# Filter MLP ahead of the modulation, and butterflies cut into an even and an odd part

## The chip, the cores and the metric

The kernel runs on one core of one Trainium2 chip. Its time is device time in microseconds; the time before is the median of three runs.

## The reference

One inference step of a two-layer backbone of width 1024 over 1024 sample tokens and 128 prompt tokens. Layer 0 mixes with gated linear attention and retention, layer 1 with a Hyena long convolution and a gated linear recurrence. Each layer's input is an RMSNorm of the tokens, scaled and shifted by a modulation that comes from the conditioning vectors (`silu(cond) @ w_mod + b_mod`).

The part that matters here is the Hyena filters. A small MLP (33 position features, then 64 and 64 hidden units, each with a sine) gives hidden units at every tap; a last layer and an exponential window make four filters of 1024 channels:

```python
def long_conv(u, hf_fwd, hf_bwd, skip):
    uf = jnp.fft.rfft(u, n=2 * L, axis=1)
    y = jnp.fft.irfft(uf * (hf_fwd + jnp.conj(hf_bwd))[None], n=2 * L, axis=1)[:, :L]
    return y + u * skip
```

The filters depend on weights alone, not on tokens, so the kernel works out their spectra first.

## The kernel before

The kernel runs in phases: phase 0 the filters' spectra, the modulation and layer 0's normalised input; phase 1 layer 0's heads; phase 2 its output projection; phase 3 layer 1's convolutions and recurrence; phase 4 its output projection. Every phase but 0 is unchanged.

A tiling framework turns the traced program into one instruction list per engine. It keeps dependences, and orders what is ready by priority, which is the order of the trace unless `high_priority(n)` lifts a block. So an instruction can move ahead of one traced earlier, but on the chip each engine then runs its list in order. `issue_after(ins)` adds an edge: every instruction that the block traces on the engine of `ins` comes behind `ins`; instructions on other engines are free. DMAs are issued from the lists of SP, ACT or POOL.

Phase 0 starts with small loads on SP (`setup`, `windows`, `mlp_loads`, `filter_weights`, `vectors`). `mlp_loads` brings the MLP's vectors (hv), its first weights (w1), the features (ft) and its second weights (w2). `filter_mlp` multiplies them (tiles `tr` in PSUM), reduces the argument on VectorE in `fold` (tiles sv, sk) and takes sines on ScalarE (tiles g); the high and low parts go to GA and GB. `table` places a load of an activation table set behind all sines. `vectors` loads a table of columns, transposes it on TensorE and copies it on VectorE (cols). `modulation` is a generator: each step multiplies one slab of w_mod (loaded from POOL into seven buffers, wm and wr); twelve steps run here, and others are put between the leaves later. `windows` makes 18 exponentials of [128, 256] (win) for each group of 256 channels.

`filters` then treats eight convolutions n (four channel groups, two filters each). For one convolution, `taps` makes 18 blocks of [128, 256] in nine PSUM tiles (`mm`, four banks in rotation, products wa x GA and wb x GB) and multiplies each by the window into `fa` on VectorE. The sum and the difference of the halves of fa, and then `butterfly`, all on VectorE, make 16 leaves: the even ones (k = 0, 2, 4, 6; k = 8 is the prompt's and needs no butterfly) from the sums, the odd ones (k = 1, 3, 5, 7) from the differences (fd). Then nine `leaf` products (mm<-fa,fw: eight TensorE instructions each) are evicted by ScalarE to fH and stored to h_dram by SP. The taps of convolution n + 1 are traced between the butterfly and the leaves of n.

Beside this, `others[n]` runs in four convolutions: n = 0 `start` (squares of nine tiles of tokens, loaded from ACT's queue into xs, for the norm's scale), n = 1, 2 and 7 `h_tiles` of three token tiles each (load x, scale, transpose on TensorE, modulate to htmp, split into hh and hl). Between leaves, in all but n = 1, one or two steps of the modulation are placed.

Of the kernel before, what the change touches and what calls it, by code (L numbers as in the profile page):

```python
# [17 lines left out]
P = 128  # L18
# [28 lines left out]
# rows of the column table: name -> (first column, number of columns)  # L47
# [18 lines left out]
def constants():  # L66
    """Arrays that depend on shapes alone."""
# [35 lines left out]
    # prompt: length 256  # L103
# [65 lines left out]
class Step:  # L169
# [53 lines left out]
    def sto2(self, out, in_):  # L223
        """a store that no load waits behind"""
        return self.nc.gpsimd.dma_start(out, in_)
# [5 lines left out]
    def rstd(self, pool, ms, shape, tag, scale=1.0):  # L231
        """(ms * scale + eps) ** -0.5 with one Newton step"""
        v = self.t(pool, shape, tag + "v")
        r = self.t(pool, shape, tag + "r")
        q = self.t(pool, shape, tag + "q")
        self.ts(v, ms, scale, OP.mult, EPS, OP.add)
        self.act(r, v, AF.Ln)
        self.act(r, r, AF.Exp, scale=-0.5)
        self.tt(q, r, r, OP.mult)
        self.tt(q, q, v, OP.mult)  # L240
        self.ts(q, q, -0.5, OP.mult, 1.5, OP.add)
        self.tt(r, r, q, OP.mult)
        return r

# [25 lines left out]
    def vectors(self, p, ps):  # L270
        """the table of columns"""
# [23 lines left out]
    def silu_sig(self, a, l, x):  # L295
        """a = sigmoid(x) = exp(min(x, 0) - ln(1 + exp(-|x|)))"""
# [7 lines left out]
    def modulation(self, layer, p, psm, js=(0, 8), more=None):  # L304
        """columns js (by 384) of the modulation as rows, and its columns once the scales are there"""
# [49 lines left out]
    def gate_row(self, layer, r, p, ps, tag="po", gate=None):  # L355
        """the gate along every partition, [P, D]"""
# [16 lines left out]
    def norm_tile(self, p, x, junk, out, tag="n"):  # L373
        """out = x * rstd"""
# [5 lines left out]
    def mod_transpose(self, ps, layer, t, xn, dst):  # L380
        """dst [P, KT, P] = (xn * A + B)^T"""
# [16 lines left out]
    def fold(self, p, v, out, tag):  # L398
        """out = sin(v); v is lost"""
# [8 lines left out]
    def table(self, name, after):  # L408
        """one load of an activation table set, behind the instructions `after`"""
# [8 lines left out]
    def mlp_loads(self, pt):  # L418
# [7 lines left out]
        self.ld(w1, i["hy_w1"][0])  # L426
        self.ld(ft, i["k_feat"])
        w2 = self.t(pt, [P, 2, 64], "w2")
        for e in range(2):
            self.ld(w2[64 * e:64 * e + 64], i["hy_w2"][0].unsqueeze(1).to_broadcast([64, 2, 64]))  # L430
        return hv, w1, ft, w2

    def filter_mlp(self, p, pt, ps, loads):
        """the hidden units of the filters' MLP at all taps, for products in two passes: their high
        and low parts on top of each other, and the high parts on rows of ones. A last block has
        the first tap alone, which only the forward filter takes."""
# [29 lines left out]
        for e in range(2):  # L466
            h = slice(64 * e, 64 * e + 64)
            for c in range(2):
# [10 lines left out]
                for z, (a, b) in enumerate(((lo, min(hi, DEC)), (DEC, hi))):  # L479
                    if a >= b:  # L480
                        continue
                    # taps a .. b - 1, then in reverse behind a first one of zero
# [8 lines left out]
    def butterfly(self, p, L, xe, xo, C):  # L491
        """the radix-16 stage: L = (the odd leaves c1, c3, c5, c7; the two of c0 and c8, then c2, c4, c6)
        from the even and odd inputs [P, 8, C]; xe may be the odd leaves' place"""
        L, E = L
# [12 lines left out]
        stt(E[:, 6:8], mp, -R2, M, d4[:, 0:4:2], A)  # L507
        w1 = self.t(p, [P, 4, C], "bs")
# [22 lines left out]
    def leaf(self, out_r, out_i, L, k):  # L531
# [9 lines left out]
        # FSIGN > 0: (C, S, -S) ; else (C, -S, -C)  # L541
# [9 lines left out]
    def windows(self, pt, g):  # L551
# [4 lines left out]
        delta = self.t(pt, [P, C], "delta")  # L556
        self.ld(delta, self.i["k_delta"][:, g * C:(g + 1) * C])
        self.win = self.t(pt, [P, 18, C], "win")
        for q in range(18):
            self.act(self.win[:, q], delta, AF.Exp, scale=self.negt[:, q:q + 1])  # L560

    def filter_weights(self, pt, n, g, o):
        """the window (once per channel group) and the last layer's weights in parts"""
# [27 lines left out]
    def filters(self, p, pi, pt, G, ps, w, others, first, rest):  # L591
        """spectra of both long convolutions, to h_dram [conv, block, f, 20 x 128]"""
        C = 256

        def taps(w):
            """the windowed taps [P, 18, C] of one convolution and channel group; the skip is a part
            of the first tap"""
# [12 lines left out]

        todo = [(g, o) for g in range(D // C) for o in range(2)]
        a = taps(w)
        self.load_fw(p)
        for n, (g, o) in enumerate(todo):
            d = self.t(pi, [P, 8, C], "fd")
            self.tt(d, a[:, 0:8], a[:, 8:16], OP.subtract)
            s = a[:, 0:8]
            self.tt(s, a[:, 0:8], a[:, 8:16], OP.add)
            L = (a[:, 0:8], a[:, 8:16])
            prompt = a[:, 16:18]  # L620
            self.butterfly(pi, L, s, d, C)
            if n + 1 < len(todo):
                a = taps(self.filter_weights(pt, n + 1, *todo[n + 1]))
            if n in others:
                others[n]()
            for k in (0, 8, 1, 2, 3, 4, 5, 6, 7):
# [5 lines left out]
                if k < 8:  # L632
                    self.leaf(pm[:, :C], pm[:, C:], L, k)
                else:
                    for e in range(2):
# [4 lines left out]
                self.nc.scalar.copy(H[:, :, :2].rearrange("p b r c -> p r b c"),  # L640
                                    pm.rearrange("p (r b c) -> p r b c", r=2, b=2))
# [4 lines left out]
                self.h_store(o, g, 0 if k == 0 else 3 if k == 8 else 4 + 2 * k, H[:, :, :m])  # L646
            for z in first:
# [12 lines left out]
    def phase0(self):  # L660
# [5 lines left out]
        with ExitStack() as st:  # L666
            po = self.pool(st, "p0o", side="right")
            self.table("natural_log_exp_and_others", [])
            self.setup(po)
# [7 lines left out]
            s2 = ExitStack()  # L677
            pa = self.pool(s2, "p0a")
            self.windows(pt, 0)
            loads = self.mlp_loads(pa)  # L680
            w = self.filter_weights(pt, 0, 0, 0)
            with self.tc.high_priority(200):
                G = self.filter_mlp(pt, pa, pst, loads)
            self.vectors(pa, pst)
            first = self.modulation(0, po, psm, (0, 6), pa)
            for z in range(12):
                next(first)
            ctx = self.st.enter_context(self.tc.issue_after(self.table("natural_log_exp_and_others", self.sins).ins))

# [38 lines left out]
    def wload(self, p, src, n, width=256, tag="w", bufs=2):  # L728
        """src [D, n] -> its two float32r parts [P, KT, n], in pieces of 128 columns"""
# [9 lines left out]
    def mm3(self, out, a, b, n=KT):  # L739
        """out = sum_k a_k^T b_k for a, b each (high, low); the product of the low parts is below  # L740
        float32's last place"""
# [7 lines left out]
    def proj_et(self, ps, w, e0, ne, evac, chunks=range(3)):  # L749
        """[e, t] products: evac(chunk, psum [ne, CH])"""  # L750
# [6 lines left out]
    def phase1(self):  # L757
        i = self.i
        with ExitStack() as st:
# [21 lines left out]
            # the low-rank gates' parts on top of each other: high, low, high  # L781
# [70 lines left out]
    def proj_te(self, w, t):  # L852
        """psum [t, e] of a tile of 128 tokens"""
# [5 lines left out]
    def gate_logs(self, hh):  # L859
        """GLA: -16 (b - b_mid) for both directions, and the tiles' decays"""  # L860
# [38 lines left out]
    def gates(self, logs, q, k):  # L899
        """GLA: q and k times exp(+-(b - b_mid)) for both directions"""  # L900
# [15 lines left out]
    def decays(self, hh, q, k):  # L916
        """retention: q with the decays since the tile's start in both directions"""
# [12 lines left out]
    def sweeps(self, h, qk, scal, v):  # L930
        """the states ahead of every tile in both directions, as the products with q take them"""
# [747 lines left out]
```

## Time and profile before

| | |
|---|---|
| median of three runs | 2481.63 us (2478.56 to 2486.62) |
| profiled execution, first to last instruction | 2485.6 us |
| mean granted clock of TensorE | 0.991 |
| busy: TensorE, VectorE, ScalarE | 2418.8, 1660.5, 1070.5 us |
| phase 0, to the first unbroken products of layer 0 | 294.55 us |

The profiled execution is one of its own; its span is given, no other time. In the rows PE is TensorE's matmuls, PEld its weight loads, DVE VectorE, ACT ScalarE, SP the queue that issues most DMAs; a name with q (SPq, ACTq) is the issue of a DMA. PEclk is the granted clock of TensorE, 1.00 for 2.4 GHz and 0.50 for 1.2 GHz. A releaser is what ended an engine's wait.

### The profile page before, as it was taken

The page shows a single profiled execution, that of the slowest core. Times are in us where ns is not written, and L with a number is a line of the kernel's source. Part 1 is how long each engine was busy: PE and PEld are TensorE (multiplying, and loading weights), DVE is VectorE, ACT ScalarE, POOL GpSimd, SP SyncE. Part 2 cuts the span into 40 slices and gives each one's busy share as a digit, 9 for nine tenths or more (in the row PEclk, how much of TensorE's full clock was granted, in tenths as well). Part 3 has the DMA queues.
Part 4 walks back from the last instruction along what each step waited for, and adds up shares of the span by engine and source line. Part 5 has one row for each costly group of instructions (what it writes and reads, how often), then busy time and mean ns, then how long its engine had stood idle before and what let it go on. Part 6 is the DMA issues. An engine that isn't in the chain of part 4 may idle for free.

```text
span 2485.6 us, 38498 instructions
## 1 busy us (share of the span) xinstructions
PE 2418.8 (97%) x14681; PEld 2203.3 (89%) x14681; DVE 1660.5 (67%) x3970; ACT 1070.5 (43%) x2355; POOL 72.6 (3%) x149
## 2 busy tenths in 40 slices
PE   5899999999999999999999999999999999999998
PEld 2766899999999999998887999999999999998786
DVE  6887568677665465473324788888888887888632
ACT  5653556465544343353233322222222227888311
POOL 2011000000000000000000000000000000000000
PEclk8999999999999999999999999999999999999999
DMA  8677521121221221144335322122212211114431
GB/s 255 201 216 217 169 58 48 42 57 46 58 58 38 53 64 41 56 124 151 108 122 162 118 62 78 50 68 70 71 57 68 65 53 52 62 62 143 155 99 42
DMA packets 201080, 230.68 MB, mean 93 GB/s; under 512 B 13823, under 2 KB 171743, under 8 KB 200448
## 3 DMA queue, kind: packets, MB, share of 16 engines
q1 hardware_dynamic: 188496, 175.24, 23.3%
q0 software_dynamic: 11104, 48.27, 6.0%
q10 hardware_dynamic: 1296, 4.72, 0.6%
q8 instruction: 115, 1.88, 0.3%
q14 instruction: 69, 0.57, 0.1%
HBM read 172.27 MB, written 55.91 MB: 92 GB/s over the span
## 4 chain that ended last, share of the span: by engine, by line
PE 85%; DVE 6%; ACT 4%; DMA 4%; issue 1%; SPq 0%; DVEq 0%; ACTq 0%
PE pp L211 44%; PE po L211 13%; PE mm L211 5%; PE X L211 5%; PE pd L211 5%; PE o L211 3%; PE tr L215 2%; PE kv L211 2%; PE pg L211 2%; PE mod L211 1%; PE sc L211 1%; PE kv L215 1%; DMA wr<-h_dram 1%; DVE cs L200 1%; DVE cs L888 1%
## 5 line engine op out<-in xcount | busy, mean ns | idle before, releaser
L211 PE MATMUL pp<-gh,wh 128*128 128x384 f32 x1152 | 390.9, 340 | 3.1 <-ACT gh L394 2.5
L211 PE MATMUL pp<-gh,wl 128*128 128x384 f32 x1152 | 392.1, 341 | 0.0
L211 PE MATMUL pp<-gl,wh 128*128 128x384 f32 x1152 | 390.6, 339 | 0.4 <-DVE gl L200 0.4
L211 PE MATMUL pp<-wh,hh 128*128 128x256 f32 x1152 | 332.7, 289 | 0.0
L211 PE MATMUL pp<-wh,hl 128*128 128x256 f32 x1152 | 328.7, 285 | 0.0
L211 PE MATMUL pp<-wl,hh 128*128 128x256 f32 x1152 | 326.2, 283 | 0.0
L211 PE MATMUL po<-woh,yth 128*128 128x512 f32 x558 | 222.7, 403 | 2.9 <-ACT woh L394 2.8
L211 PEld LDWEIGHTS pp<-wh,hl 128*128 128x128 f32 x1152 | 221.7, 192 | 0.0
L211 PEld LDWEIGHTS pp<-gh,wh 128*128 128x128 f32 x1152 | 216.7, 188 | 4.5 <-ACT gh L394 3.1
L211 PEld LDWEIGHTS pp<-wl,hh 128*128 128x128 f32 x1152 | 220.6, 192 | 0.0
L211 PE MATMUL po<-wol,yth 128*128 128x512 f32 x558 | 220.1, 395 | 0.1
L211 PEld LDWEIGHTS pp<-wh,hh 128*128 128x128 f32 x1152 | 220.2, 191 | 0.0
L211 PE MATMUL po<-woh,ytl 128*128 128x512 f32 x558 | 218.8, 393 | 1.0 <-DVE ytl L200 1.0
L211 PEld LDWEIGHTS pp<-gh,wl 128*128 128x128 f32 x1152 | 216.7, 188 | 0.8
L211 PEld LDWEIGHTS pp<-gl,wh 128*128 128x128 f32 x1152 | 216.3, 188 | 1.2 <-DVE gl L200 0.7
L200 DVE TENSOR_TENSOR wl<-wr,wh 128x1024 fp32r<-128x1024 f32 (+1 forms) x97 | 118.0, 1217 | 120.2 <-ACT wh L394 119.5
L394 ACT CAST wh<-wr 128x1024 fp32r<-128x1024 f32 (+1 forms) x97 | 101.4, 1045 | 138.9 <-PE pp L211 138.8
L211 PEld LDWEIGHTS mm<-fa,fw 128*128 128x128 f32 x576 | 104.8, 190 | 41.1 <-issue 13.1
L211 PE MATMUL mm<-fa,fw 128*128 128x256 f32 x576 | 138.7, 388 | 0.0
L211 PE MATMUL pp<-hh,wh 128*128 128x384 f32 (+1 forms) x408 | 136.6, 335 | 0.3 <-ACT htmp L197 0.3
L211 PE MATMUL pp<-hh,wl 128*128 128x384 f32 (+1 forms) x408 | 136.7, 335 | 0.0
L211 PE MATMUL pp<-hl,wh 128*128 128x384 f32 (+1 forms) x408 | 136.5, 335 | 0.0
(323 smaller groups left out, 4892.2 us busy)
## 6 DMA issues: line engine op xcount, KB each, us to landing
wr<-in_ab_w_in_dram SPq DMA_DIRECT2D x48, 512.0 KB
wr<-in_cd_w_in_dram SPq DMA_DIRECT2D x48, 512.0 KB
H<-h_dram SPq DMA_DIRECT2D x32, 640.0 KB
wr<-in_w_mod_dram POOLq DMA_DIRECT2D x49, 384.0 KB, 4.6
h_dram<-fH SPq DMA_DIRECT2D x112, 128.0 KB
y_dram<-y SPq DMA_DIRECT2D x72, 128.0 KB
y<-y_dram SPq DMA_DIRECT2D x36, 256.0 KB
x<-in_x_sample_dram SPq DMA_DIRECT2D x16, 512.0 KB
```

Source lines behind the costliest of these rows:

```text
L200: return self.nc.vector.tensor_tensor(out=out, in0=a, in1=b, op=op)
L211: self.last_mm = self.nc.tensor.matmul(out, l, r, start=start, stop=stop)
L215: return self.nc.tensor.transpose(out, in_, self.ident)
L394: self.nc.scalar.copy(hi, x)
L888: self.nc.vector.tensor_tensor_scan(x, self.ones, x, 0.0, OP.mult, OP.add)
```

## The change

The loads of the MLP are traced first of all, and w1, ft and w2 are issued from ACT's queue. The load of the transform's matrices (fw, 1856 KB) moves from behind the first taps to ahead of the columns' and biases' loads. On TensorE the columns' transposition and the first twelve modulation steps come behind the MLP's last product. Of the first 18 windows, six are made at the start and twelve behind the table load that follows the sines.

The butterfly is two functions. In `filters`, the sums and the even part come first, then the leaves 0, 8, 2, 4, 6; then the differences and the odd part, the next convolution's taps, the other work (on ScalarE behind the last even leaf's eviction), and the leaves 1, 3, 5, 7. The even leaves now live in fd, the odd ones in fa. Elsewhere only comments go. The other use of the butterfly, in the long convolution, calls the two parts in turn.

```diff
@@ mlp_loads
-        self.ld(w1, i["hy_w1"][0])
-        self.ld(ft, i["k_feat"])
+        ld = self.nc.scalar.dma_start
+        ld(w1, i["hy_w1"][0])
+        ld(ft, i["k_feat"])
         w2 = self.t(pt, [P, 2, 64], "w2")
         for e in range(2):
-            self.ld(w2[64 * e:64 * e + 64], i["hy_w2"][0].unsqueeze(1).to_broadcast([64, 2, 64]))
+            self.last_ld = ld(w2[64 * e:64 * e + 64], i["hy_w2"][0].unsqueeze(1).to_broadcast([64, 2, 64]))
@@ butterfly
-    def butterfly(self, p, L, xe, xo, C):
-        L, E = L
+    def butterfly(self, p, L, x, C):
+        self.butterfly_even(p, L[1], x, C)
+        self.butterfly_odd(p, L[0], x, C)
+
+    def butterfly_even(self, p, E, xe, C):
         tt, stt = self.tt, self.stt
...
         stt(E[:, 2:4], mp, R2, M, d4[:, 0:4:2], A)
         stt(E[:, 6:8], mp, -R2, M, d4[:, 0:4:2], A)
+
+    def butterfly_odd(self, p, L, xo, C):
+        tt, stt = self.tt, self.stt
+        A, S, M = OP.add, OP.subtract, OP.mult
         w1 = self.t(p, [P, 4, C], "bs")
         w3 = self.t(p, [P, 4, C], "bd")
...
@@ windows
-        for q in range(18):
-            self.act(self.win[:, q], delta, AF.Exp, scale=self.negt[:, q:q + 1])
+        self.window(0, 18 if g else 6)
+
+    def window(self, a, b):
+        for q in range(a, b):
+            self.act(self.win[:, q], self.delta, AF.Exp, scale=self.negt[:, q:q + 1])
@@ filters
         todo = [(g, o) for g in range(D // C) for o in range(2)]
         a = taps(w)
-        self.load_fw(p)
         for n, (g, o) in enumerate(todo):
-            d = self.t(pi, [P, 8, C], "fd")
-            self.tt(d, a[:, 0:8], a[:, 8:16], OP.subtract)
-            s = a[:, 0:8]
-            self.tt(s, a[:, 0:8], a[:, 8:16], OP.add)
-            L = (a[:, 0:8], a[:, 8:16])
-            prompt = a[:, 16:18]
-            self.butterfly(pi, L, s, d, C)
+            E = self.t(pi, [P, 8, C], "fd")
+            L = a[:, 0:8]
+            prompt = a[:, 16:18]
+            self.tt(E, a[:, 0:8], a[:, 8:16], OP.add)
+            self.butterfly_even(pi, E, E, C)
+            evac = leaves(n, g, o, (0, 8, 2, 4, 6), E, L, prompt)
+            self.tt(L, a[:, 0:8], a[:, 8:16], OP.subtract)
+            self.butterfly_odd(pi, L, L, C)
             if n + 1 < len(todo):
                 a = taps(self.filter_weights(pt, n + 1, *todo[n + 1]))
             if n in others:
-                others[n]()
-            for k in (0, 8, 1, 2, 3, 4, 5, 6, 7):
+                with self.tc.issue_after(evac.ins):
+                    others[n]()
+            leaves(n, g, o, (1, 3, 5, 7), E, L, prompt)
             for z in first:
                 pass
@@ phase0
             self.table("natural_log_exp_and_others", [])
+            s2 = ExitStack()
+            pa = self.pool(s2, "p0a")
+            loads = self.mlp_loads(pa)
             self.setup(po)
...
-            s2 = ExitStack()
-            pa = self.pool(s2, "p0a")
             self.windows(pt, 0)
-            loads = self.mlp_loads(pa)
             w = self.filter_weights(pt, 0, 0, 0)
-            with self.tc.high_priority(200):
+            self.load_fw(p)
+            with self.tc.high_priority(200), self.tc.issue_after(self.last_ld.ins):
                 G = self.filter_mlp(pt, pa, pst, loads)
-            self.vectors(pa, pst)
-            first = self.modulation(0, po, psm, (0, 6), pa)
-            for z in range(12):
-                next(first)
+            with self.tc.issue_after(self.last_mm.ins):
+                self.vectors(pa, pst)
+                first = self.modulation(0, po, psm, (0, 6), pa)
+                for z in range(12):
+                    next(first)
             ctx = self.st.enter_context(self.tc.issue_after(self.table("natural_log_exp_and_others", self.sins).ins))
+            self.window(6, 18)
```

The new inner function `leaves(n, g, o, ks, E, L, prompt)` is the old body of the loop over k, for the leaves ks; it returns the last eviction.

## Rows read from the trace of the kernel before

**Rows 1.** The page, part 1: busy time, share of the span and instructions by engine.
```profile
PE 2418.8 (97%) x14681; PEld 2203.3 (89%) x14681; DVE 1660.5 (67%) x3970; ACT 1070.5 (43%) x2355; POOL 72.6 (3%) x149
```

**Rows 2.** Busy time by stretch, phase 0: PE, PEld, DVE, ACT, POOL, clock, DMA share, GB/s.
```profile
0.00:42.60 42.60, 24.04 (x82) 8.71 (x82) 20.78 (x58) 21.86 (x54) 13.26 (x30) 0.94 0.85 271
42.60:72.00 29.40, 14.66 (x66) 13.90 (x66) 27.43 (x44) 14.12 (x29) 0.00 (x0) 0.62 0.69 201
...
101.00:167.70 66.70, 60.16 (x312) 44.53 (x309) 53.61 (x79) 50.97 (x110) 6.86 (x14) 0.97 0.64 194
167.70:256.00 88.30, 88.30 (x453) 58.18 (x454) 69.14 (x114) 31.34 (x64) 17.27 (x34) 1.00 0.73 223
```

**Rows 3.** Timeline, 0 to 44 us: start, us, engine, line, operation, out<-in, count [idle before <-releaser].
```profile
2.32 0.43 SPq L218 DMA_DIRECT2D delta<-in_k_delta_dram  x1
...
5.83 0.39 SPq L218 DMA_DIRECT2D ft<-in_k_feat_dram  x1
...
7.92 6.87 ACT L197 ACTIVATE win<-delta,negt 128x256 f32<-128x256 f32 x17
...
12.94 2.18 PE L211 MATMUL tr<-ft,w 33*64 33x288 f32 x8 [1.81 <-DMA ft<-in_k_feat_dram]
...
19.32 0.78 ACT L197 ACTIVATE g<-sv 128x288 f32<-128x288 f32 x2
...
30.17 0.29 DVE L293 COPY cols<-tr 128x128 f32<-128x128 f32 x1 [2.25 <-PE tr L215]
...
40.59 1.28 ACT L410 ACT_TABLE_LOAD   x1
...
43.39 0.29 ACT L453 CAST GB<-g 64x127 fp32r<-64x127 f32 x1
```

**Rows 4.** Timeline, 48 to 73 us, VectorE and TensorE, the first butterfly.
```profile
48.38 0.69 DVE L200 TENSOR_TENSOR fa<-mm,win 128x512 f32<-128x512 f32 x1 [0.41 <-PE mm L211]
...
51.31 2.29 DVE L200 TENSOR_TENSOR fa<-fa 128x2048 f32<-128x2048 f32 x1
...
53.52 0.68 DVE L200 TENSOR_TENSOR wb<-raw,wi 128x512 fp32r<-128x512 f32 x1
...
54.90 0.58 PE L211 MATMUL mm<-wb,GB 128*128 128x256 f32 x1 [5.39 <-ACT wb L588]
...
56.39 1.29 DVE L200 TENSOR_TENSOR fa<-bs 128x512 f32<-128x512 f32 x2
...
66.44 4.39 DVE L200 TENSOR_TENSOR fa<-mm,win 128x512 f32<-128x512 f32 x7
67.17 0.58 PE L211 MATMUL mm<-wa,GA 128*128 128x256 f32 x1 [8.91 <-DVE fa L200]
...
72.85 1.99 PE L211 MATMUL mm<-fa,fw 128*128 128x256 f32 x8
```

**Rows 5.** The chain that ended last, 180 to 345 us: start, us, what.
```profile
190.12 6.79 PE mm L211 x48
196.90 0.77 PE mod L211 x4
...
200.37 1.92 PE mm L211 x8
...
294.55 12.66 PE pp L211 x73
```

**Rows 6.** Instructions of the tile xs: duration min/median/max in ns, first and last start.
```profile
L197 ACT ACTIVATE xs<-xs x9: 1052/1057/1061, 45.5 to 70.0; 128x1024 f32<-128x1024 f32 x9
```

**Rows 7.** Waits of TensorE, 72 to 168 us: us in total, times, longest.
```profile
PE tr L215 <- ACT x L197: 3.9, 5, 1.4
```

**Rows 8.** Timeline, 277 to 291 us: the last tile of tokens.
```profile
277.02 0.40 SPq L218 DMA_DIRECT2D x<-in_x_prompt_dram  x1
...
283.60 1.09 PE L215 MATMUL tr<-ident,x 128*128 128x128 f32 x8 [0.38 <-ACT x L197]
...
289.91 1.22 DVE L200 TENSOR_TENSOR hl<-htmp,hh 128x1024 fp32r<-128x1024 f32 x1 [4.17 <-ACT hh L394]
```

More of the change, by code (lines that the diff above doesn't have):

```diff
@@ L555, in windows @@
             self.ld(self.negt, self.i["k_negt"])
-        delta = self.t(pt, [P, C], "delta")
-        self.ld(delta, self.i["k_delta"][:, g * C:(g + 1) * C])
+        self.delta = self.t(pt, [P, C], "delta")
+        self.ld(self.delta, self.i["k_delta"][:, g * C:(g + 1) * C])
         self.win = self.t(pt, [P, 18, C], "win")
-        for q in range(18):
-            self.act(self.win[:, q], delta, AF.Exp, scale=self.negt[:, q:q + 1])
+        self.window(0, 18 if g else 6)
+    def window(self, a, b):
+        for q in range(a, b):
+            self.act(self.win[:, q], self.delta, AF.Exp, scale=self.negt[:, q:q + 1])
     def filter_weights(self, pt, n, g, o):
@@ L609, in taps, with leaves @@
             return a
-        todo = [(g, o) for g in range(D // C) for o in range(2)]
-        a = taps(w)
-        self.load_fw(p)
-        for n, (g, o) in enumerate(todo):
-            d = self.t(pi, [P, 8, C], "fd")
-            self.tt(d, a[:, 0:8], a[:, 8:16], OP.subtract)
-            s = a[:, 0:8]
-            self.tt(s, a[:, 0:8], a[:, 8:16], OP.add)
-            L = (a[:, 0:8], a[:, 8:16])
-            prompt = a[:, 16:18]
-            self.butterfly(pi, L, s, d, C)
-            if n + 1 < len(todo):
-                a = taps(self.filter_weights(pt, n + 1, *todo[n + 1]))
-            if n in others:
-                others[n]()
-            for k in (0, 8, 1, 2, 3, 4, 5, 6, 7):
+        def leaves(n, g, o, ks, E, L, prompt):
+            for k in ks:
                 if n != 1:
@@ L632, in filters @@
                 if k < 8:
-                    self.leaf(pm[:, :C], pm[:, C:], L, k)
+                    self.leaf(pm[:, :C], pm[:, C:], (L, E), k)
                 else:
@@ L639, in filters @@
                 H = self.t(p, [P, 2, 3, P], "fH", bufs=3)
-                self.nc.scalar.copy(H[:, :, :2].rearrange("p b r c -> p r b c"),
-                                    pm.rearrange("p (r b c) -> p r b c", r=2, b=2))
+                evac = self.nc.scalar.copy(H[:, :, :2].rearrange("p b r c -> p r b c"),
+                                           pm.rearrange("p (r b c) -> p r b c", r=2, b=2))
                 if m == 3:
@@ L646, in filters @@
                 self.h_store(o, g, 0 if k == 0 else 3 if k == 8 else 4 + 2 * k, H[:, :, :m])
+            return evac
+        todo = [(g, o) for g in range(D // C) for o in range(2)]
+        a = taps(w)
+        for n, (g, o) in enumerate(todo):
+            E = self.t(pi, [P, 8, C], "fd")
[6 more added lines that the diff above has]
+            self.butterfly_odd(pi, L, L, C)
+            if n + 1 < len(todo):
+                a = taps(self.filter_weights(pt, n + 1, *todo[n + 1]))
+            if n in others:
+                with self.tc.issue_after(evac.ins):
+                    others[n]()
+            leaves(n, g, o, (1, 3, 5, 7), E, L, prompt)
             for z in first:
@@ L1549, in long_conv @@
         L = [x, self.wide(p, "L1")]
-        self.butterfly(self.ph, L, x[:, 0:8], x[:, 0:8], P)
+        self.butterfly(self.ph, L, x[:, 0:8], P)
         Da, Db = [self.wide(p, f"D{e}") for e in range(2)]
```

## The prediction

> **What bounds the kernel now.** The page's first part comes first: TensorE is busy for 97% of the span [rows 1]. That share is a mean over stages, and the change touches one stage, the filters' spectra (phase 0, up to 294.5 us). So the second view is busy time by stretch [rows 2]. From 167.7 to 256 us TensorE is busy without a gap at full clock: there the stage is bound by TensorE, and VectorE (69 of 88 us) has room. From 42.6 to 72 us it is the reverse: VectorE 27.4 of 29.4 us, TensorE 14.7 at a granted clock of 0.62. From 0 to 42.6 us neither is full. In 101 to 167.7 us some 6.5 us of TensorE are missing. What can be won lies ahead of 72 us; after that only lost time of a few us.
>
> Third, the timeline says who is late. Ahead of 42 us it is the chain of the filters' MLP [rows 3]: its feature load is issued at 5.83, its first product starts at 12.94, the first sines at 19.32, the last table change at 40.59. From 48 to 73 us it is VectorE's first butterfly [rows 4]: the last taps of convolution 0 end at 49.07, the first leaf starts at 72.85, and TensorE's wait of 8.91 us ends on the taps' multiply behind the butterfly.
>
> **The MLP ahead, its start.** w1, the features and w2 leave SP for ACT's queue; behind a table load of 1.28 us [rows 3] and one issue of some 0.4 us I put the features' issue at 2.4 instead of 5.83. The product could then start about 7 us earlier. But the sines need their table, and six window exponentials come first. They need delta: before it was issued at 2.32 and the windows ran by 7.92 (5.6 us) [rows 3]; now the four vector loads stand ahead of it. Delta to features is 3.5 us for four such loads and one more, so some 2.7 us: delta at 5.0, landed 10.5. Six windows at 6.87/17 = 0.40 us are 2.4, the table 1.28: sines at 14.3 instead of 19.32, -5. Bounds: -7 (products set it) and -2 (the first weight cast, waiting for its load, stays in front of the sines).
>
> The Trainium skill, DMA: Bandwidth & Descriptors, "Issuing engines are not separate DMA queues", says that transfers from several engines run on the same 16 DMA engines, and that another issuer saves only issue time. By it the features keep their 7.1 us from issue to use under the modulation's loads and the product starts at 9.5, so sines at 15 to 16 and a sum about 1 us smaller than mine; the trace has no load on this queue as early as that.
>
> **The MLP ahead, its middle.** From the first sines to the last table 21.3 us pass. VectorE does the range reduction and in it stands still for 2.25 us ahead of the columns' copy [rows 3], because the transposition of the columns sits on TensorE behind modulation products. Now both come behind the MLP's last product on TensorE. I take -3 (the wait, the copy and its twin); bounds -5 and 0 (fw, 1.9 MB, is now issued ahead of the columns' loads, so these land later and could hold TensorE, the modulation behind them, and the taps). The modulation's twelve first steps lose their place beside the MLP; TensorE waits at that time for VectorE anyway, and without that cover they cost some 12 x 0.8 us. Their loads go on as before, on POOL's queue.
>
> **The windows behind the sines.** Twelve of 18 exponentials now follow the table change: casts of the last chunk end 43.39 + 0.29 - 40.59 = 3.1 us behind its start, then 12 x 0.40 = 4.9, then one multiply of 0.69: 8.7 us. Before, the last multiply ended at 49.07, 8.5 us behind that start [rows 3, 4]. So 0; bound +4.9 if windows come ahead of the casts. Taps 0 end at 41 instead of 49.
>
> **The split.** Before: 72.85 - 49.07 = 23.8 us to the first leaf. Now the first leaf needs one sum of 2.29 us and the first pair of even outputs: from 51.31 to 57.03 in [rows 4], less the weight part run in between (53.52, 0.6 us to the next), 5.1 us. That is 18.7 less. But the second convolution's taps, done in that time, now come behind the even leaves: 6.79 - 1.92 = 4.9 us [rows 5]. Left 13.8. The first leaves meet TensorE at 0.62 [rows 2]; taps 1 paid this before, 4.9 us of work at half clock (67.17 to 72), so -2.4. And taps 1 may slip into the 5 us gap, as they did at 54.90 [rows 4], and hold some of four banks until VectorE comes to them: -2. That makes 9. Bounds: 13.8 and 0 (all banks held). In the later convolutions it gives nothing: nine leaves of 1.92, nine modulation steps of 0.77 and 4.9 us of taps are 29.1 us [rows 5], and VectorE's 69 us for three of them hide behind it; even leaves cover the odd part, odd leaves the next sums. The operations, the long convolution's too, are the same in number and size.
>
> **What is pushed behind the even leaves.** The other work of convolutions 0, 1, 2 and 7 now waits on ACT for the even leaves' last eviction. In convolution 0 this is the squares of nine token tiles and their loads, both on ACT's queue: 45.5 to 71.2 us before, hidden under the butterfly [rows 6]. Now: first leaf 41 + 5.3 = 46.3, even leaves 5 x 2.7 + 2.4 + 2 = 18, eviction at 65, first load landed some 4 us later, the chain of 25.8 us over at 95. Queued behind it on ACT: the evictions of odd leaves, windows, the scaling of token tiles, whose transpositions TensorE meets behind taps 2. TensorE gets there at 64.3 + 4.9 + 4 x 2.7 + 5 x 1.92 + 4.9 = 94.5. So the cover ends just there. Before, the same kind of wait took 3.9 us in five pieces [rows 7]. I take +3; bounds 0 and +12.
>
> In convolution 7 the last three token tiles wait for the even leaves, 4 x 1.92 = 7.7 us ahead of the stage's end. A tile takes 5.3 us of load and 1.3 of scaling (277.02 to 283.60), 1.1 of transposition, and from transposition to last part 7.5 [rows 8]; loads wait for the buffer, so three take 2.4 + 2 x 7.7 + 6.4 = 24, some 16 us past the end. The first layer's gate products on the other two chunks are 48 x 0.173 = 8.3 us [rows 5]; the 8 us left are idle unless the first head's products are put there. +2; bounds 0 and +8.
>
> **Sum.** -5 - 3 + 0 - 9 + 3 + 2 = -12, made against the span of 2485.6, which is 4 us above the runs' median of 2481.63; I carry the difference over: 2469.6.
>
> **Rivals.**
> A, the banks: taps 1 take all four PSUM banks in the gap, and the even leaves wait for the whole butterfly. For it: taps 1 were there 12 us early [rows 4]. Against: their weight part comes from VectorE, which now has the butterfly first. Then the split gives 0: -3, 2478.6, no measurable change.
> B, slower, the squares' chain: it decides once the scale of the tokens is ready later than about 107 us, so 12 us past TensorE's arrival. Each tile after the first then costs 7.7 us of chain with only 7.7 us of odd leaves for two of them, 8 more; with the 8 us at the end, 28 against the 17 won: +11, 2492.6. For it: each ACT wait on a load also holds evictions, and stores of spectra now run beside these loads. Against: before, in 101 to 167.7 us, with token loads and spectra stores together, TensorE lost only 6.5 of 66.7 us [rows 2].
> C, hidden anyway: the MLP comes 2 us earlier only and the columns' late loads take the rest: -2 - 9 + 5 = -6, 2475.6, within the noise.
> D, more: no banks lost, no exposure behind: -8 - 11.4 - 3 = -22, 2459, where some of the 6.5 us go too.
>
> **How the numbers follow.** About 0.3% (7.4 us) is what a measurement here can tell from no change: faster ends at 2474.2, slower begins at 2489. The forecast gets 0.50 (its own range 2464 to 2474), D 0.14, A 0.13, C 0.11, B 0.12. Faster: 0.50 + 0.14, and 0.02 of C's lower edge, 0.66; slower 0.11 of B; same the remaining 0.23. From D's end with 2 us more of bounds, 2457, to 2486 on B's near side leaves under 0.2 out.
>
> **What would show it.** In the new trace: first MLP product by 6 to 10 us, first sines near 14, table change near 32, windows directly behind it; taps 0 over near 41; first leaf near 46 with the odd part on VectorE beside the even leaves; taps 1 on TensorE behind the fifth leaf. The squares from about 69 to 95. Layer 0's products at about 282. Wrong would be: sines still behind the weight cast; leaves waiting on multiplies (A); transpositions of tokens waiting many us on ACT (B); a gap after 282 that ends on the last token tile.

## The result: slower, where a gain was forecast

Four runs of the changed kernel beside four of the kernel before: 2503.36 us (2499.16 to 2504.18) against 2481.28 (2478.56 to 2486.62). These medians are 22 us apart. The ratio, by which all runs below are compared, is 1.0074, interval 1.0062 to 1.0086, so about 18 us slower (15 to 21) where 12 us faster was forecast. The profiled execution took 2499.16 us, its span is 2497.2.

Busy time is as before [rows 1]; only the span grew.

```profile
PE 2414.1 (97%) x14681; PEld 2201.0 (88%) x14681; DVE 1660.5 (66%) x3970; ACT 1071.1 (43%) x2355; POOL 72.7 (3%) x149
```

The unbroken products of layer 0 begin at 308.05 us; before, at 294.55 [rows 5]. Busy time by stretch, columns as in [rows 2], says where the 13.5 us went:

```profile
0.00:45.80 45.80, 23.83 (x116) 10.98 (x116) 24.98 (x66) 22.91 (x59) 13.66 (x31) 1.00 0.80 260
45.80:69.00 23.20, 15.06 (x65) 8.13 (x65) 18.01 (x28) 5.95 (x13) 4.42 (x10) 0.78 0.57 166
69.00:100.00 31.00, 23.09 (x129) 19.39 (x128) 24.30 (x44) 14.48 (x28) 0.54 (x2) 0.96 0.78 246
100.00:129.60 29.60, 21.53 (x101) 18.00 (x100) 15.99 (x22) 23.27 (x55) 0.30 (x1) 0.75 0.41 133
129.60:224.80 95.20, 95.20 (x482) 62.77 (x484) 78.38 (x127) 49.23 (x104) 18.59 (x37) 1.00 0.77 230
...
266.00:308.00 42.00, 31.00 (x162) 26.63 (x161) 27.09 (x40) 23.90 (x49) 0.96 (x4) 0.89 0.58 173
```

The weak place behind the first taps is shorter (8 us of TensorE missing in 45.8 to 69, 15 in 42.6 to 72 before), and from 129.6 to 224.8 TensorE never stops. New holes are there instead: 8 us each in 69 to 100 and 100 to 129.6 (the clock at 0.75 in the second), and 11 us in 266 to 308. The list of TensorE's waits, 0 to 330 us, names them:

```profile
PE mm L211 <- DVE fd L200: 12.7, 4, 8.7
...
PE tr L215 <- ACT x L197: 7.4, 3, 6.1
PE mm L211 <- ACT fH L642: 6.1, 1, 6.1
PE mm L211 <- ACT wb L600: 5.8, 1, 5.8
```

The timeline, in the order of the prediction's steps:

```profile
1.40 0.29 ACTq L428 DMA_DIRECT2D ft<-in_k_feat_dram  x1
...
7.87 0.43 SPq L218 DMA_DIRECT2D delta<-in_k_delta_dram  x1
...
8.69 2.19 PE L211 MATMUL tr<-ft,w 33*64 33x288 f32 x8
...
15.73 0.51 ACT L197 ACTIVATE win<-delta,negt 128x256 f32<-128x256 f32 x1 [5.32 <-DMA delta<-in_k_delta_dram]
...
20.16 0.44 ACT L197 ACTIVATE g<-sv 128x288 f32<-128x288 f32 x1
...
37.97 1.28 ACT L410 ACT_TABLE_LOAD   x1
...
45.83 2.29 DVE L200 TENSOR_TENSOR fd<-fa 128x2048 f32<-128x2048 f32 x1
48.04 0.68 DVE L200 TENSOR_TENSOR fa<-mm,win 128x512 f32<-128x512 f32 x1
48.64 1.22 DVE L200 TENSOR_TENSOR bs<-fd 128x1024 f32<-128x1024 f32 x1
49.77 1.22 DVE L200 TENSOR_TENSOR bd<-fd 128x1024 f32<-128x1024 f32 x1
50.91 2.28 DVE L200 TENSOR_TENSOR fa<-fa 128x2048 f32<-128x2048 f32 x1
53.11 1.28 DVE L200 TENSOR_TENSOR fd<-bs 128x512 f32<-128x512 f32 x2
...
76.89 1.06 ACT L197 ACTIVATE xs<-xs 128x1024 f32<-128x1024 f32 x1 [2.78 <-DMA xs<-in_x_sample_dram]
...
99.61 3.78 PE L211 MATMUL mm<-fd,fw 128*128 128x256 f32 x8 [6.10 <-ACT fH L642]
...
101.69 1.06 ACT L197 ACTIVATE xs<-xs 128x1024 f32<-128x1024 f32 x1 [0.65 <-DMA xs<-in_x_prompt_dram]
...
105.48 5.69 ACT L197 ACTIVATE win<-delta,negt 128x256 f32<-128x256 f32 x14
111.20 0.61 ACT L600 CAST wb<-wi 32x512 fp32r<-32x512 f32 x1
...
111.86 0.58 PE L211 MATMUL mm<-wb,GB 128*128 128x256 f32 x1 [5.85 <-ACT wb L600]
...
279.05 1.97 PE L211 MATMUL mm<-fd,fw 128*128 128x256 f32 x8 [1.99 <-DVE fd L200]
...
303.94 1.97 PE L215 MATMUL tr<-ident,x 128*128 128x128 f32 x8 [6.09 <-ACT x L197]
...
308.05 0.63 PE L211 MATMUL pp<-hh,wh 128*96 128x384 f32 x1 [2.14 <-ACT htmp L197]
```

- **Head.** The features are issued at 1.40 and multiplied at 8.69, 4.3 us earlier than in [rows 3]. The windows wait for delta, which SP issues only at 7.87, so the first sine comes at 20.16, later than the 19.32 of before. The middle is shorter, 17.8 us to the last table load instead of 21.3.
- **First butterfly.** The even outputs that the first leaf needs (fd<-bs) come 7.3 us behind the sum's start: VectorE runs a multiply and the odd difference ahead of them (48.04 and 50.91, 2.9 us). The multiply is the ninth of convolution 0's own taps, the prompt's, which the sum does not need; before, it ran ahead of the sum, so it only changed places (0.6 us). The odd difference is what is new in between. The leaf starts at 53.94, 8.1 us behind the eighth multiply; the forecast had 5.1 behind all nine.
- **Squares.** From 76.89 to 102.8 instead of 45.5 to 71.2 [rows 6]. ACT works its list in order: behind each wait for a token load stand evictions of leaves (TensorE waits 6.10 us), then at 102.7 the 18 windows of the next channel group, then the weight cast, for which TensorE stands 5.85 us.
- **End.** The even leaves of convolution 7 start at 279.05; the last three token tiles come one after the other behind them, the last transposition 6.09 us late, and layer 0 starts at half clock (14.89 us for 72 products, 12.66 for 73 in [rows 5]; from the chain that ended last: start, us, what).

```profile
308.05 14.89 PE pp L211 x72
```

Theory 1: the loss is what stands on ACT behind the even leaves' last eviction. Theory 2: the split itself costs, by VectorE's order and TensorE's clock. Theory 3: moving the MLP ahead costs.

### The profile page after: what moved, and what is told of

It is laid out like the page before. It is cut to its first block, busy times and chain, and to the rows that moved or that the text cites. A ratio compares the mean times of both kernels' runs of the same rounds, so it can differ in the third digit from the quotient of the medians.

```text
span 2497.2 us, 38502 instructions
## 1 busy us (share of the span) xinstructions
PE 2414.1 (97%) x14681; PEld 2201.0 (88%) x14681; DVE 1660.5 (66%) x3970; ACT 1071.1 (43%) x2355; POOL 72.7 (3%) x149
## 4 chain that ended last, share of the span: by engine, by line
PE 85%; DVE 6%; ACT 4%; DMA 3%; issue 2%; SPq 0%; POOL 0%; DVEq 0%; ACTq 0%; POOLq 0%
PE pp L211 45%; PE po L211 14%; PE mm L211 5%; PE X L211 5%; PE pd L211 5%; PE o L211 3%; PE tr L215 2%; PE kv L211 2%; PE pg L211 2%; PE mod L211 1%; PE sc L211 1%; PE kv L215 1%; DVE fa L200 1%; DMA wr<-h_dram 1%; DVE cs L200 1%
## 5 line engine op out<-in xcount | busy, mean ns | idle before, releaser
L211 PE MATMUL pd<-iv,Y 128*128 128x256 f32 (+1 forms) x576 | 132.0, 370 | 0.0
L211 PEld LDWEIGHTS po<-woh,yth 128*128 128x128 f32 x558 | 104.6, 188 | 26.7 <-ACT woh L394 4.3
```

Of the source, the lines that this page charges most:

```text
L211: self.last_mm = self.nc.tensor.matmul(out, l, r, start=start, stop=stop)
```

## The experiments

All times beside runs of the kernel before on the same chip; its median there was 2482.7 to 2484.5 us, so 0.1% is 2.5 us (the changed kernel's row is the result above). The last column is the first of layer 0's unbroken products in the timeline; by this reading it is 294.20 before (294.55 in the chain of [rows 5]). The profiled execution of the kernel before was a long one: its span is 2485.6 us, and the median of its executions beside these runs is near 2482. So a gain read against 294 can come out 3 us too large.

| run | ratio to before | interval | layer 0, us |
|---|---|---|---|
| changed kernel | 1.0074 | 1.0062 to 1.0086 | 308.05 |
| mlp_alone | 0.9991 | 0.9982 to 1.000 | 289.81 |
| split_alone | 1.0058 | 1.0044 to 1.0071 | 303.79 |
| start_free | 1.0033 | 1.0021 to 1.0046 | 296.79 |
| last_free | 1.0027 | 1.0017 to 1.0037 | 297.38 |
| others_free | 0.9978 | 0.9969 to 0.9988 | 285.35 |
| split_free | 0.9984 | 0.9975 to 0.9993 | 289.97 |
| even_first | 0.9946 | 0.9932 to 0.9959 | 278.36 |
| split_even | 0.9947 | 0.9933 to 0.996 | 277.24 |
| loads_first | 0.9988 | 0.9979 to 0.9996 | 290.45 |
| others_even | 0.9986 | 0.9977 to 0.9994 | 287.81 |
| head | 0.9972 | 0.9961 to 0.9982 | 286.24 |
| head_even | 0.9964 | 0.9951 to 0.9977 | 280.95 |
| nosq_even | 0.9927 | 0.9913 to 0.9941 | 271.48 |
| nosq_split | 0.9928 | 0.9915 to 0.9941 | 272.62 |

**mlp_alone and split_alone** take the change in two: the first has the new head with the old `filters`, the second the old head with the new `filters` and butterfly.

> Only the first part of the change: the MLP's loads ahead, its products ahead of the columns and the modulation, windows in two pieces; the butterfly and its leaves as before. Theory 1 (the loss comes from what is ordered behind the even leaves): this part is a small gain, the taps of convolution 0 end 3 us earlier as in the changed kernel and nothing behind them is lost, 2478 us (2474 to 2481). Theory 3 (moving the MLP ahead costs in itself, since the windows' operand arrives at 15.7 us and modulation loses its cover): 2484 or more.

> Only the split of the butterfly, with the edges that hold the other work behind the even leaves' last eviction; the head as before. Theory 1 and theory 2 (the split itself costs, by VectorE's order and by TensorE's lower clock) both say slower than before by 15 to 25 us, 2496 to 2506; if the loss belonged to the MLP's part it would be 2472 to 2482.

The first is 2 us faster by its median (2482.33), at the edge of what the measurement tells and 1 us outside the range expected; the second carries the loss, 14 us by its ratio (2498.48 us). Theory 3 falls: by itself the MLP's part costs nothing. In mlp_alone the first sine too is late (20.74).

The two do not simply add up: -2 and +14 are 12, not 18; the intervals of split_alone and of the changed kernel overlap, so the difference is not certain. In the trace of split_alone the squares end at 105.5, later than in the changed kernel, and TensorE waits 5.5 us on an eviction, but the wait of 5.8 on the weight cast is not there: that one came with both parts together.

**others_free, last_free and start_free** take the order away: for all of the other work, for convolution 7, for convolution 0.

```diff
-                with self.tc.issue_after(evac.ins):
-                    others[n]()
+                others[n]()
```

In last_free and start_free the edge goes for n == 7 or n == 0 alone.

> The changed kernel, but the other work of convolutions 0, 1, 2 and 7 is no longer ordered behind the even leaves' last eviction. Theory 1: the squares' chain comes back beside the first butterfly, the last token tiles run beside the last convolution, at least 15 us come back: 2488 or less, and layer 0's products start by 295 us. Theory 2: most of the loss stays, 2495 or more, with TensorE waiting on VectorE's even outputs.

> The changed kernel with the edge taken from the last token tiles alone (convolution 7). Theory 1: the gap behind the last even leaves (TensorE 11 us short of full in the 42 us up to 308, and layer 0 begun at half clock) closes, 7 to 11 us come back: 2489 to 2494; the stretch from 100 to 112 us stays as in the changed kernel. Theory 2: no more than 3 us come back, 2497 or more.

> The changed kernel with the edge taken from the squares' chain alone (convolution 0). Freeing the last token tiles alone gave 2492 us, freeing all gave 2479. If the squares' chain carries the rest (theory 1), this run comes to about 2489 (13 us under the changed kernel), the gap of TensorE from 100 to 112 us is gone and the scale of the tokens is there by 85 us; the half-clock start of layer 0 stays. If the rest belongs to the token tiles of convolutions 1 and 2 instead, it stays at 2497 or more.

Without the edges the kernel is 2478.62 us; the edges cost 1.0074 - 0.9978 = 0.96%, 24 us. Convolution 0's alone is 0.41% (10 us), convolution 7's 0.47% (12 us); about 2 us are left for the other two, which no run freed alone and which lie within the intervals. Without the MLP's part the edges cost less, 18 us (split_alone 1.0058, split_free 0.9984). TensorE's waits in others_free, 0 to 330 us, no longer hold the eviction of 6.1, the cast of 5.8 (now 0.7) and the token tiles:

```profile
PE mm L211 <- DVE fd L200: 12.6, 3, 8.3
...
PE mm L211 <- ACT fH L638: 3.5, 1, 3.5
...
PE mm L211 <- ACT wb L600: 0.7, 1, 0.7
```

Theory 1 is shown: the run that takes nothing but the edges away turns the loss into a gain. What is left of the change is a gain of 5 us, not 17. start_free gave 10 us back where 13 were expected; its token tiles behind convolution 7 are as late as in the changed kernel (TensorE waits 6.1 us for the last).

**split_free and even_first** ask where the rest of the split's gain is. split_free is split_alone without the edges. even_first is others_free with one edge more, on VectorE:

```diff
-            self.tt(L, a[:, 0:8], a[:, 8:16], OP.subtract)
+            with self.tc.issue_after(self.last_even.ins):
+                self.tt(L, a[:, 0:8], a[:, 8:16], OP.subtract)
```

(last_even is the last operation of `butterfly_even`.)

> The split without its edges and without the MLP's part (the head as before). The prediction's term was a gain of 9 us, 2475 us. Theory 2 in its smaller form (the split gives less, since VectorE puts a multiply of taps 1 and the odd difference ahead of the even outputs, and TensorE is at half clock when the leaves come): a gain of 2 to 6 us, 2478 to 2482. A split that gives nothing: 2484 or more.

> The kernel without the edges, with the odd part's difference ordered on VectorE behind the last even output. If VectorE's order is what the first leaf waits for, the first leaf comes 2.3 us earlier (51 instead of 53.2 us), and TensorE's waits on the even outputs fall from 12.6 to 10 us or less: 2476 us, so near the uncertainty of the time that the trace decides. If the even outputs wait for something else, the first leaf stays at 53.

split_free gives 4 us (0.9984), less than half of the 9 forecast. (The multiply that its expectation gives to taps 1 is the ninth of convolution 0, as said above.) even_first gives 0.32% (8 us) more than others_free where 2 to 3 were expected (2476 us). VectorE in even_first, with its first leaf:

```profile
44.30 2.29 DVE L200 TENSOR_TENSOR fd<-fa 128x2048 f32<-128x2048 f32 x1
...
49.38 0.68 DVE L200 TENSOR_TENSOR wb<-raw,wi 128x512 fp32r<-128x512 f32 x1
49.98 1.29 DVE L200 TENSOR_TENSOR fd<-bs 128x512 f32<-128x512 f32 x2
...
50.81 3.75 PE L211 MATMUL mm<-fd,fw 128*128 128x256 f32 x8 [7.13 <-DVE fd L200]
...
53.18 2.28 DVE L200 TENSOR_TENSOR fa<-fa 128x2048 f32<-128x2048 f32 x1
```

The difference now runs beside the leaves, and the first leaf comes 2.4 us earlier than in others_free (53.20). The price was not only there: in others_free the same order stood ahead of later even leaves, where TensorE waited 2.22 us in convolution 2 (118.74) and 2.04 in convolution 7 (267.36). TensorE's waits in even_first, 0 to 310 us:

```profile
PE mm L211 <- DVE fd L200: 8.2, 3, 7.1
PE tr L446 <- DMA sc<-in_c_ctx_dram: 7.9, 1, 7.9
PE mm L211 <- ACT fH L638: 4.0, 2, 3.6
```

The waits on even outputs fell by 4.4 us against others_free, 1.2 of them at the first leaf and 3.2 behind it, and its 2.2 us for the modulation's weights and 1.9 us for windows are down to 0.2 and nothing. Theory 2 holds in its smaller form as far as VectorE's order goes. Its other half, the clock, no run varied: the first leaf took 3.75 us in even_first too, where a later one takes 1.99.

**split_even, others_even, head.** split_even is split_free with the same edge, so the whole without the MLP's part. others_even is even_first with the other work written ahead of the even leaves. head is others_even with the loads at the start in another order (ident, condition, time column and delta, then the vectors and second weights, all on SP; w1 and the features on ACT) and the first weight casts behind the second sine:

```diff
 (others_even)
+            if n in others:
+                others[n]()
             evac = leaves(n, g, o, (0, 8, 2, 4, 6), E, L, prompt)
...
-            if n in others:
-                others[n]()
 (head)
+            self.mlp_vectors(loads)
+            with self.tc.issue_after(self.sins[1].ins):
+                w = self.filter_weights(pt, 0, 0, 0)
+            self.load_fw(p)
```

> The split alone (head as before, no edges), with the odd part's difference behind the last even output. The prediction's term for the split was -9 us. With VectorE's order as it came, the split alone gave 4 to 5 us. If VectorE's order took the rest, this gives 8 to 12 us: 2473 to 2477, and no wait on the even outputs above 1 us in the later convolutions. If the order matters only together with the earlier MLP, it stays at 2478 or more.

> The kernel without the edges and with the difference behind the even outputs (2470.6 us), the other work now written ahead of the even leaves instead of behind the taps, so that the modulation's bias no longer takes the token tiles' buffer ahead of the last of them. If that buffer still costs, tiles 3 to 5 are all done by 165 us and 1 to 3 us come back, 2468 to 2470. If not, since TensorE is busy for all of 130 to 225 us anyway, no change: 2470 to 2472. If the squares now hold the first even evictions, worse: 2474 or more.

> As the run beside it, and the head reordered: the loads of ident, the condition, the time column and delta first on SP, then the MLP's vectors and second weights, the features on ACT's queue; the first weights' casts behind the second sine. The prediction's term for an earlier start of the MLP was -5 us. If the order of loads and ACT's list (windows, silu, first cast) held the sines, the first sine comes at 13 to 15.5 us instead of 20.2 and the time falls by 3 to 5 us against the run beside it, to 2464 to 2467. If the loads of TensorE's modulation or fw take it back before the taps, the taps of convolution 0 still end at 44 to 46 us and the time stays.

split_even is 2470.17 us, a gain of 13 us, a little over the 8 to 12 expected: 0.37% (9 us) under split_free, and as fast as even_first (2470.55) with the MLP's part. TensorE's waits on even outputs, behind the first leaf, in split_free and in split_even, 0 to 330 us:

```profile
PE mm L211 <- DVE fd L200: 6.1, 3, 2.2
...
PE mm L211 <- DVE fd L200: 0.4, 2, 0.3
```

others_even came out as the last of its three cases: 10 us slower than even_first. Its squares stand ahead of the even leaves' evictions, and ACT's wait of 3.26 us for a token load holds one of them and TensorE for 5.99:

```profile
73.95 1.06 ACT L197 ACTIVATE xs<-xs 128x1024 f32<-128x1024 f32 x1 [3.26 <-DMA xs<-in_x_sample_dram]
...
75.01 0.34 ACT L642 COPY fH<-mm 1x256 f32<-1x256 f32 x1
...
75.41 0.58 PE L211 MATMUL mm<-wa,GA 128*128 128x256 f32 x1 [5.99 <-ACT fH L642]
```

even_first has such a stop too, of 3.62 us, so this is 2.4 of the ten. TensorE also waits 3.2 instead of 1.1 us for token tiles, and the first leaf starts 2.2 us later (53.05); the rest was not followed, and no run moved the squares alone. head has its first sine at 14.92, 5.4 us earlier than others_even, and is 3 us faster than it (0.9972, with intervals that touch).

**loads_first** is others_free with the time column and delta loaded ahead of the vectors.

```diff
+            self.window_loads(pt, 0)
             loads = self.mlp_loads(pa)
```

> The kernel without the edges, with the loads of the windows' operands (the time column and delta) issued ahead of the MLP's vector loads. If the windows' late operand is what takes the gain of the MLP's start, ACT no longer stands 5.4 us ahead of the first window, the first sine comes at 15 to 17 us instead of 20.2 and the time falls by 3 to 5 us, to 2474 to 2476. If another wait is just behind it (the first weight cast, the products' own loads that now come later), the first sine stays after 18.5 and the time at 2477 or more.

Its second case came: 2481.63 us, 0.1% slower than others_free. The windows start at 9.25 and the first sine at 18.62, 1.5 us earlier only: ACT then stood 4.32 us for the first weight cast's load, and the sigmoid of the condition, now behind the first sine, cost two more table changes of 1.28 us.

```profile
16.07 0.62 ACT L602 CAST wa<-raw 128x512 fp32r<-128x512 f32 x1 [4.32 <-DMA raw<-in_hy_w_dram]
...
18.62 0.44 ACT L197 ACTIVATE g<-sv 128x288 f32<-128x288 f32 x1
```

**head_even, nosq_even, nosq_split** ask why the MLP's part gives nothing on top of the good split. head_even is even_first with head's start. nosq_even and nosq_split are even_first and split_even with the squares of the token tiles and their loads left out; the tokens' scale comes from a constant, so they show times alone.

```diff
-                for t in range(NT):
-                    x = self.t(pa, [P, D], "xs", bufs=2)
-                    self.nc.scalar.dma_start(x, self.x_src(t))
-                    self.act(x, x, AF.Square, accum_out=ss[:, t:t + 1])
+                self.nc.gpsimd.memset(ss, 1024.0)
```

> The best kernel so far with the MLP's part (no edges, difference behind the even outputs) with the squares of the nine token tiles and their loads left out, the sums set to a constant. If the MLP's lead of 3 us at the first leaf is given back because ACT's list waits for these tiles' loads and holds the evictions (4.8 and 1.8 us between 66 and 76 us), taps 1 now run through without the stop at 69 to 73 us, and this run is 2 to 4 us under its twin without the MLP's part, phase 0 over by 273 us. If the lead is lost elsewhere, the twins stay equal.

> The twin: the split alone in the same order, with the squares and their loads left out. First leaf near 53.7 us as with them. If the squares' chain swallowed the MLP's lead, this one is 2 to 4 us slower than the run with the MLP's part; if not, within 1.5 us of it.

> The reordered head (first sine at 14.9 us instead of 20.2, last table change at 36.9) on the best order of the rest: no edges, difference behind the even outputs, the other work behind the taps. If a lead at the head reaches the end, 3 us under the same without the reordered head, 2467 to 2468. If it is swallowed by the token loads on ACT behind the first leaves, no change: 2469.5 to 2472.

In even_first the taps of convolution 1 start at 66.48 and stop until 72.69 [3.62 on an eviction]; in split_even they start at 68.87, 2.4 us later, and go on at 73.12. The second convolution's even leaves come at 87.87 and 86.53: the lead is gone. Without the squares the stop is gone in both. But there the lead was smaller from the start (first leaf 52.57 and 52.84, second 57.78 and 58.94); 1.1 us were left of it at the end of the stage (271.48 and 272.62), and the times are equal (2464.97 and 2464.54). So a lead of 1 us gets through to layer 0 where the stop is not; a gain of 1 us in time is below what these runs can tell. Where the 2.4 us go, the traces of even_first and split_even tell: behind the stop 0.4 of them are left (72.69 and 73.12), and at the first odd leaf even_first is 0.8 us behind (78.99 and 78.22); TensorE's granted clock from 73 to 79 us is 0.52 in even_first and 0.72 in split_even. The squares and their loads together cost some 5 us (0.9946 against 0.9927). head_even missed, 4 us slower than even_first (0.9964): its first sine is 5 us earlier (15.11 and 19.78), its taps not, since a multiply of the first taps now stands on VectorE ahead of the range reduction and waits for TensorE:

```profile
29.32 0.69 DVE L200 TENSOR_TENSOR fa<-mm,win 128x512 f32<-128x512 f32 x1 [2.86 <-PE mm L211]
...
32.70 0.44 ACT L197 ACTIVATE g<-sv 128x288 f32<-128x288 f32 x1 [4.87 <-DVE sv L205]
...
39.15 0.58 PE L211 MATMUL mm<-wa,GA 128*128 128x256 f32 x1 [3.97 <-DVE GA L200]
```

## Why the prediction was wrong, by its own steps

By the runs the change is the sum of three: the MLP -2 us (mlp_alone), the split -4 (split_free), the edges +24, together +18, which is what was measured. The 24 contain what the parts cost together: without the MLP's part the edges cost 18. The forecast had -8, -9 and +5. The miss of 30 us is 10 in the last tiles, 7 in the squares, 6 in the MLP's part, 5 in the split, and 2 for the edges of convolutions 1 and 2, for which the forecast had no term.

- **Squares, +3: a mis-sized term, 10 us.** The step took TensorE's meeting with the token tiles' transpositions as the place where the chain decides, and priced it by [rows 7]. It named what is queued behind the squares on ACT (odd evictions, windows) and gave that no price. There the time went: 6.1 us on an eviction and 5.85 on a cast behind 18 windows, both ahead of the first transposition (117.6 us). The chain ended at 102.8 instead of 95. Rival B had the chain and its outcome, at +11, but its point of decision (107 us for the scale) was wrong for the same reason: the scale was there by 105 us (the last square ended at 102.8), and the loss came all the same.
- **Last tiles, +2: the second mis-sized term, 12 us.** The chain was worked out right: 24 us behind the edge were forecast, and from the last even eviction (over at 288.7) to the last part of the third tile (310.3) it took 21.7. The step that failed is its cover. The gate products on the other two chunks, 8.3 us, were to run in that time, and of 8 us more, "idle unless the first head's products are put there", it took 2. Neither stands there: on TensorE all of these products come behind the last tile's transposition, so it waited 6.09 us for that and 2.14 for ACT to read it, and the layer began at 1.2 GHz, 2.4 us more over 72 products.
- **MLP's start, -5: it was +0.8.** The step "delta at 5.0, landed 10.5" failed. The chain that ended last (start, us, what) begins with SP waiting until the second vector load has landed, and with delta behind it, landed at 15.6:

```profile
1.56 5.89 DMA hv<-in_hy_freq_dram
7.87 7.77 DMA delta<-in_k_delta_dram
```

   The Trainium skill, DMA: Bandwidth & Descriptors, "Issuing engines are not separate DMA queues", says that a second issuer saves issue time alone. The trace does not contradict it, and does not show it either: the features' product starts 7.3 us behind their issue, 7.1 before, but here TensorE's last wait was for ident (until 8.33), so the features may have landed earlier. The step counted issue time alone; in the trace of the kernel before, too, SP stood 0.9 us (6.22 to 7.13) with eleven loads issued. Delta was the first thing in the way and the weight cast the next: with delta early but the cast in place the first sine came at 18.62 (loads_first), with both moved at 14.92 (head).
- **MLP's middle, -3: right,** 3.5 us; windows behind the sines, 0: right (40.97 to 45.9, directly behind the casts). Rival C's "2 us earlier only" is what mlp_alone measured; the cause that it gave, the columns' late loads, is not the one found.
- **Split, -9: 4 as written, 13 in the order that the step assumed.** "one sum of 2.29 us and the first pair of even outputs", 5.1 us, left out the odd difference, which VectorE ran ahead of these outputs. In even_first, with the difference behind, the first leaf starts 6.5 us behind the sum, and 1.2 of them are the ninth multiply and a weight part: the 5.1 was right for that order. With the difference behind, split_even gives 0.53%, 13 us, near the 13.8 ahead of the two deductions. Of these the clock's was there (the first leaf at 3.75 us), the banks' was not. Rival A did not come: taps 1 start at 70.6, behind the fifth leaf, and held no banks before.
- **Later convolutions, 0: the larger part of the split's miss.** The step said that "even leaves cover the odd part, odd leaves the next sums". In split_free TensorE waited 6.1 us on even outputs behind the first leaf (1.9 in convolution 1, 2.2 in 2, 2.0 in 7), in split_even 0.4; at the first leaf itself 1.6 us less (7.45 and 5.84). So more was lost in these three convolutions than in the first butterfly. The changed kernel has such waits at 86.36 (1.80) and 279.05 (1.99).

Open: why the edges cost 6 us more together with the MLP's part than without it, beyond the wait on the weight cast that only the whole change has; whether the order of the squares alone makes others_even slow; why taps and leaves start up to 2 us apart from one kernel to the next (50.81 in even_first, 52.57 in nosq_even).

## What to carry over

Ordering work behind an instruction orders everything that its engine's list holds after it: price each thing queued there, not only the consumer of the moved work. When a stage is split for an earlier start, read the order on the engine that feeds the first piece; one operation of the second piece ahead of it, in four convolutions, took more than half of the gain (9 of 13 us). Work that has to be done by the stage's end must not wait for its last piece: behind it, TensorE has nothing to do and its clock falls. The fastest orders here, even_first and split_even, beat the kernel before by 0.5%.

## What the runs showed of the hardware

- Two issuing engines did not get more loads through at the head. With nine loads issued by 4.5 us, seven from SP and two from ACT, SP stood until 7.47 us, when the second vector load had landed, and ACT's issue of the second weights came at 7.67; before, SP alone had issued eleven by 6.22 and stood until 7.13.
- Idle TensorE costs twice: after the stop at 106 to 112 us the granted clock was 0.75 over 100 to 129.6 (products of taps took 0.41 us until 117.6 and 0.28 from 118), and 72 products of layer 0 behind the wait at 308 took 14.89 us, where 73 took 12.66 before.
- A table change of 1.28 us comes with each switch between sine and exponential: with the sigmoid split by one sine (loads_first) three stood at 17.32, 19.08 and 20.60.
